# Moving the norm factors of the memory's rows into the second projection chunk of a hybrid decoder layer

## The chip, the cores and the metric

The kernel runs on one core of a Trainium2 chip. Time is device time in microseconds (us). A core has five engines that run side by side, each in the order of its own instructions: TensorE (PE; PEld is its weight load), VectorE (DVE), ScalarE (ACT), GpSimd (POOL) and SyncE (SP), which here only issues DMAs. They wait for each other by semaphores.

## What is computed

One decoder layer on 1024 tokens of width 1024, in float32:

```
h = x + w_out [ DSA-sparse-attention(groupA) ; DiffAttn(groupB) ](rmsnorm(x) @ w_in)
h = h + CrossAttn(rmsnorm(h), rmsnorm(mem))      # 4 heads, 256 memory tokens
h = h + ConvGLU(rmsnorm(h))

def rmsnorm(x, g):
    y = xf * lax.rsqrt(jnp.mean(xf * xf, axis=-1, keepdims=True) + EPS)
    return y * g

def cross_attention(hn, memn, w_xq, w_xk, w_xv, w_xo, g_xq, g_xk):
    k = rmsnorm((memn @ w_xk).reshape(B, M, X_HEADS, X_HEAD_DIM), g_xk)
    v = (memn @ w_xv).reshape(B, M, X_HEADS, X_HEAD_DIM)
```

The memory `mem` has 256 rows of width 1024. What the change is about are the factors 1/sqrt(mean of squares + eps) of these rows, one for each.

## The kernel before

Tokens and memory rows lie 128 to a tile, one on each partition. The input projection runs in column chunks: chunk 0 (0 to 48 us), chunk 1 (to about 106 us; its loop over eight token tiles calls `proj_mm(1, t)` and `c1_post`, `c1_tr`, which build the keys of group A and of the index heads), and chunks 2 to 4 (to about 264 us). Each product is three matmuls, L308 to L310, on a split of the operands, and ScalarE evacuates the sum at L646. The split of a weight tile `raw` is made at L201 and L204.

Then comes the differential attention ("B phase", 264 to 480 us), in units of one head and one block of 128 queries. A unit is a chain over the engines: GpSimd splits the queries (`hl`, L738, L739), TensorE transposes them (L746), ScalarE evacuates (`qbs`, L748), TensorE makes the logits (L766, L767), VectorE masks and takes the maximum (`e`, `st`, L774), ScalarE takes the exponential (L776), VectorE combines the two softmaxes (reciprocal L784, L785, L786), TensorE transposes the result (L691), ScalarE evacuates (`pt`, L682), and TensorE multiplies by the values (L797). Into the units are put the key and value products of the memory (`mem_mm`, L885; evacuation `mem_evac`, L889, which scales by the row factors `rm`; `memk_post` with the Square L894, the reduce L896, `rstd` on VectorE and two products with `gkq` at L900), and steps of the top-k search of group A (L553 on ScalarE, L555 to L571 on VectorE). After it come group A's attention (to 650 us), the cross-attention and the ConvGLU.

Except in the ConvGLU, a scheduler that follows a timeline of its own sets the order of the instructions on each engine; no order is written by hand around the change. Buffers come from rings: `rt("t2")` has three, the pool `early` has five of tag "xr" and closes when tile 2 of chunk 1 is reached. The search steps are issued by `tick` at a pace, behind the last evacuations; that is so in both kernels.

The row factors before: `mem_prep`, called as the B phase opens, loads the two memory tiles of 512 KB (L873) on SP's queue and takes ScalarE's Square with its sum, `ssm` (L875); two loads of the gain vectors (`gx`, L877, L878) follow, whose product `gkq` GpSimd makes (L879). At step -2 of the B loop GpSimd's `rstd` turns `ssm` into `rm` (L107, L108, L118 to L127, twelve steps). VectorE's form of `rstd` has nine (L107 to L116). All of them work on two columns.

Of the kernel before, what the change touches and what calls it, by code (L numbers as in the profile page):

```python
# [9 lines left out]
F32 = mybir.dt.float32  # L10
F32R = mybir.dt.float32r
BF = mybir.dt.bfloat16
I32 = mybir.dt.int32
AF = mybir.ActivationFunctionType
# [4 lines left out]
P = 128  # L19
T = 1024  # L20
D = 1024
# [17 lines left out]
def rows(ap, n=P):  # L39

    return bass.AP(tensor=ap.tensor, offset=ap.offset, ap=[[0, n]] + [list(d) for d in ap.ap])
# [3 lines left out]
def hybrid_layer(ctx, tc, I, out):  # L45
    nc = tc.nc
    pe, act, dve, pool, sp = nc.tensor, nc.scalar, nc.vector, nc.gpsimd, nc.sync

    def open_pool(name, **kw):
        st = ExitStack()  # L50
        p = st.enter_context(tc.tile_pool(name=name, bufs=1, reuse_waits="tile", **kw))
        return st, p
# [8 lines left out]
    def nm(s):  # L61
        cnt[0] += 1
        return f"{s}_{cnt[0]}"

    def ctile(shape, dt, name):
        return const.tile(shape, dt, name=name)
# [10 lines left out]
    def accp():  # L77
        return ps.tile([P, 512], F32, name=nm("acc"), tag="acc", bufs=2)

    def small(name, shape=(P, 8), bufs=8):  # L80
        return wpool.tile(list(shape), F32, name=nm(name), tag=name, bufs=bufs)
# [8 lines left out]
    rm = ctile([P, 2], F32, "rm")  # L90
# [7 lines left out]
    ssm = ctile([P, 2], F32, "ssm")  # L98
# [3 lines left out]
    def rstd(eng, r, ss, n, scale):  # L102


        w = small("rst", (P, 3, 8), 4) if n <= 8 else rt("hl", [P, 3, 64], F32, "rstw")
        m, y, t = w[:, 0, :n], w[:, 1, :n], w[:, 2, :n]
        eng.tensor_scalar(m, ss, scale, EPS, op0=OP.mult, op1=OP.add)  # L107
        eng.tensor_scalar(y.bitcast(I32), m.bitcast(I32), -0.5, 1597463007.0, op0=OP.mult, op1=OP.add)  # L108
        if eng is dve:
            eng.scalar_tensor_tensor(t, y, -3.0 / 16, y, op0=OP.mult, op1=OP.mult)  # L110
            eng.tensor_tensor(t, t, m, op=OP.mult)
            eng.scalar_tensor_tensor(y, t, 9.0 / 16, y, op0=OP.add, op1=OP.mult)
            eng.scalar_tensor_tensor(t, y, 64.0 / 9, y, op0=OP.mult, op1=OP.mult)
            eng.tensor_tensor(t, t, m, op=OP.mult)
            eng.scalar_tensor_tensor(t, t, -10.0 / 3, t, op0=OP.add, op1=OP.mult)
            eng.scalar_tensor_tensor(r, t, 5.0, y, op0=OP.add, op1=OP.mult)  # L116
        else:
            eng.tensor_tensor(t, y, y, op=OP.mult)  # L118
            eng.tensor_tensor(t, t, m, op=OP.mult)
            eng.tensor_scalar(t, t, -3.0 / 16, 9.0 / 16, op0=OP.mult, op1=OP.add)  # L120
            eng.tensor_tensor(y, t, y, op=OP.mult)
            eng.tensor_tensor(t, y, y, op=OP.mult)
            eng.tensor_tensor(t, t, m, op=OP.mult)
            eng.tensor_scalar(m, t, 64.0 / 9, -10.0 / 3, op0=OP.mult, op1=OP.add)
            eng.tensor_tensor(t, t, m, op=OP.mult)
            eng.tensor_scalar(t, t, 64.0 / 9, 5.0, op0=OP.mult, op1=OP.add)
            eng.tensor_tensor(r, t, y, op=OP.mult)  # L127
# [179 lines left out]
    def mm3(o, lh, ll, rh, rl, start, stop):  # L307
        pe.matmul(o, lhsT=lh, rhs=rh, start=start, stop=False)  # L308
        pe.matmul(o, lhsT=lh, rhs=rl, start=False, stop=False)  # L309
        pe.matmul(o, lhsT=ll, rhs=rh, start=False, stop=stop)  # L310
# [13 lines left out]
    def rt(tag, shape, dt, name):  # L324
        return rot.tile(shape, dt, name=nm(name), tag=tag, bufs=ROT[tag])

    ROT = {"X": 3, "t2": 3, "tb": 2, "kk2": 2, "hl": 2, "qt": 2}
    qa_d = tc.dram_tile([T, 512], F32, name="qa_d")
# [11 lines left out]
    early_st, early = open_pool("early")  # L340
    ki_t = [kq([P, T], F32R, "ki") for j in range(2)]

    for tag, n in (("X", 512), ("t2", 512), ("hl", 512), ("tb", 256), ("kk2", 256), ("qt", 128)):
        rt(tag, [P, n], F32, tag)
# [16 lines left out]
    for k in range(KT):  # L361
# [11 lines left out]
        for t in (C1_ORDER if k == KT - 1 else range(NT)):  # L373
            s = slice(t * P, (t + 1) * P)
            mm3(pj0[t][:, :452], h[:, s], l[:, s], w0[k][:, 0, :452], w0[k][:, 1, :452], k == 0, k == KT - 1)
        if k == 0:
# [5 lines left out]
            for j, g in enumerate(("g_ka", "g_qa", "g_qb", "g_kb")):  # L382
                sp.dma_start(gv[:, j, :], rows(I[g]))
            lamv = rt("X", [P, 4, 64], F32, "lamv")
            for j, g in enumerate(("lam_q1", "lam_k1", "lam_q2", "lam_k2")):
# [8 lines left out]
    for t in range(NT):  # L394
        xt = early.tile([P, T], F32, name=nm("xraw"), tag="xr", bufs=5)
        sp.dma_start(xt, I["x"][t * P:(t + 1) * P, :])
        jk = rt("t2", [P, T], BF, "jk")
# [6 lines left out]
    dve.tensor_scalar(gs[:, :, 0:32], gv[:, :, 32:64], -1.0, None, op0=OP.mult)  # L404
    ang = rt("X", [P, NT, 32], F32, "ang")
    kk = rt("hl", [P, NT, 32], F32, "kk")
# [23 lines left out]
    for j in range(2):  # L430
        dve.scalar_tensor_tensor(lt, lamv[:, 2 * j, :], 1.0, lamv[:, 2 * j + 1, :], op0=OP.mult, op1=OP.mult,
                                 accum_out=misc[:, j:j + 1])
# [34 lines left out]
    def c1_evac(t):  # L467
        if t % 2 == 0:
            c1x[t // 2] = early.tile([P, 2, 512], F32, name=nm("c1x"), tag="xr", bufs=5)
        X = c1x[t // 2][:, t % 2, :]  # L470
        act.activation(X[:, :452], pj0[t][:, :452], AF.Copy, scale=rx[:, t:t + 1])
        act.activation(X[:, 452:484].bitcast(BF), X[:, 0:64], AF.Square, accum_out=rka[:, 0, t:t + 1])
# [166 lines left out]
    def proj_mm(c, t):  # L639
        pages = W.get(("in", c), 8)  # L640
        p = accp()
        s = slice(t * P, (t + 1) * P)
        for k in range(KT):
            mm3(p, xh[k][:, s], xl[k][:, s], pages[k][:, 0, :], pages[k][:, 1, :], k == 0, k == KT - 1)
        X = rt("X", [P, 512], F32, "X")
        last["act"] = act.activation(X, p, AF.Copy, scale=rx[:, t:t + 1])  # L646
        return X
# [80 lines left out]
    def b_load_q(u):  # L728
        h, i = b_units[u]
        qt = rt("qt", [P, 2, 64], F32, "qt")  # L730
        sp.dma_start(qt.rearrange("p c d -> p (c d)"), qk_d[h // 2][i * P:(i + 1) * P, (h % 2) * 128:(h % 2) * 128 + 128])
        b_q[u] = qt
# [55 lines left out]
    def b_t(u):  # L788
        h, i = b_units[u]
        b_pt[u] = p_transposes(b_e[u][0][0], i + 1)  # L790
# [21 lines left out]
    store = None  # L812
    idxq = [lambda t=t, h=h: idx_head(t, h) for t in range(2, NT) for h in range(4)]
    mb, sc = {}, {}
    for t in range(NT):
        X = proj_mm(1, t)
        if t == 2:
            early_st.close()
            scp_st, scp = open_pool("scp")
            for i in range(2, NT):  # L820
                mb[i] = scp.tile([P, P * (i + 1)], BF, name=f"mb{i}")
                sc[i] = scp.tile([P, P * (i + 1)], F32, name=f"sc{i}")
        if t == 7:
            W.free(8)
        W.pump(2 if t == 3 else 1)
        for a in steps[t]:
            if a == "i":
                idxq.pop(0)()
            else:
                (c1_post if a[0] == "p" else c1_tr)(int(a[1]))  # L830
        if store:
            store()
        store = proj_post(1, t, X)
# [24 lines left out]
    def etile(name):  # L858
        return obp.tile([P, T], F32, name=nm(name), tag="e", bufs=4)
# [7 lines left out]
    def mem_prep():  # L867
        pages = W.get("memT", 2)
        for j in range(KT):
            mstat[j] = pages[j // 4].bitcast(F32)[:, j % 4 // 2, (j % 2) * 256:(j % 2) * 256 + 256]  # L870
        for t in range(2):
            xt = etile("mtok")
            sp.dma_start(xt, I["mem"][t * P:(t + 1) * P, :])  # L873
            jk = rt("t2", [P, T], BF, "jk")
            act.activation(jk, xt, AF.Square, accum_out=ssm[:, t:t + 1])  # L875
        gx = rt("t2", [P, 2, 256], F32, "gx")
        sp.dma_start(gx[:, 0, :], rows(I["g_xq"]))  # L877
        sp.dma_start(gx[:, 1, :], rows(I["g_xk"]))  # L878
        pool.tensor_tensor(gkq, gx[:, 0, :], gx[:, 1, :], op=OP.mult)  # L879
# [70 lines left out]
    for s in range(-4, NB):  # L950
        h, i = b_units[max(s, 0)]
        m = s % NT

        def ok(u):
            return 0 <= u < NB
        if s % 4 == 0:
            if s >= 0:
                b_acc[s // 4] = accp()
        if s + 5 >= 2 and ok(s + 5):
            b_load_q(s + 5)  # L960
        if s >= 0 and h < 3 and m == 1:
            b_load_k(h + 1)
            b_load_v(h + 1)
        if ok(s + 4):
            b_split(s + 4)
        if s == -2:
            rstd(pool, rm, ssm, 2, 1.0 / D)
        if ok(s + 3):
            b_qt(s + 3)
        if ok(s):  # L970
            b_t(s)
        if ok(s + 2):
            b_s(s + 2)
        mem_step(MB)
        if ok(s + 1):
            b_comb(s + 1)
        if s >= 0 and h < 3 and 2 <= m <= 5:
            b_k(h + 1, (m - 2) // 2, 4 * (m % 2))
        if ok(s):
            b_av(s)  # L980
            W.pump(1)
            tick(0.8 + 0.85 * (i + 1))
# [753 lines left out]
```

## Time and profile before

| what | us |
|---|---|
| median of 3 runs (lowest to highest) | 1662.94 (1659.94 to 1664.27) |
| the profiled execution, its time | 1662.24 |
| the profiled execution, its span | 1660.4 |
| TensorE busy (share) | 1572.2 (95%) |
| VectorE busy (share) | 1208.5 (73%) |
| ScalarE busy (share) | 803.7 (48%) |
| GpSimd busy (share) | 639.1 (38%) |
| granted TensorE clock, mean | 0.978 |

The rows that follow further down come from this one profiled execution. A busy share is an average over stages: the ConvGLU stages keep TensorE full, and its waits lie in the first 480 us. What counts for the change are two stretches, the entry to the B phase (264 to 302 us), where code is taken out, and chunk 1 (50 to 82 us), where it is put in.

### The profile page before, as it was taken

What the parts mean: (1) busy time and instruction counts of PE and PEld (TensorE: products, weight loads), DVE (VectorE), ACT (ScalarE), POOL (GpSimd) and SP (SyncE); (2) the same over time, 40 slices, a digit from 0 to 9 for tenths busy, and PEclk for the clock granted to TensorE, in tenths of its full rate; (3) what the DMA queues carried; (4) which work ended last, traced back from release to release, by engine and by line L of the source; (5) the groups of instructions that cost most, each with busy time, mean ns of one, the idle gap of its engine ahead of it and who ended that gap; (6) DMA issues with size and microseconds to landing.
All of it is one profiled execution on the core that took longest, in us unless ns stands there. A gap on an engine that the chain in (4) does not pass through costs nothing.

```text
span 1660.4 us, 22257 instructions
## 1 busy us (share of the span) xinstructions
PE 1572.2 (95%) x7596; PEld 1271.6 (77%) x7596; DVE 1208.5 (73%) x2356; ACT 803.7 (48%) x1696; POOL 639.1 (38%) x888
## 2 busy tenths in 40 slices
PE   8899898888789999999999997999999999999999
PEld 7788675666668888878777775888887777888887
DVE  5738888878868875345544379989999999855554
ACT  6556665677877446428442265433333333343432
POOL 2735776223351131031101023666666666551111
PEclk9999998989989999999999998999999999999999
DMA  8320236221210122152203121455555555799812
GB/s 284 102 83 32 91 128 216 77 78 47 64 64 27 52 96 70 67 181 102 89 1 114 40 97 57 167 191 179 176 180 180 183 184 179 262 361 366 305 52 76
DMA packets 112162, 220.06 MB, mean 133 GB/s; under 512 B 18480, under 2 KB 38448, under 8 KB 112048
## 3 DMA queue, kind: packets, MB, share of 16 engines
q1 hardware_dynamic: 91072, 148.37, 26.7%
q0 software_dynamic: 18384, 61.36, 10.4%
q10 hardware_dynamic: 2592, 8.91, 1.4%
q8 instruction: 60, 0.98, 0.2%
q14 instruction: 54, 0.44, 0.1%
HBM read 160.92 MB, written 57.67 MB: 132 GB/s over the span
## 4 chain that ended last, share of the span: by engine, by line
PE 68%; DVE 16%; DMA 6%; ACT 4%; issue 3%; POOL 2%; SPq 0%; ACTq 0%; POOLq 0%; DVEq 0%
PE acc L308 11%; PE acc L310 10%; PE acc L309 10%; PE big L309 4%; PE big L308 4%; PE big L310 4%; PE trp L308 3%; PE trp L309 3%; PE trp L310 3%; PE acc L1036 3%; PE acc L885 2%; DVE jk L565 2%; DVE wp L204 2%; PE trp L691 2%; PE big L1275 2%
## 5 line engine op out<-in xcount | busy, mean ns | idle before, releaser
L204 DVE TENSOR_TENSOR wp<-raw,wp 128x512 fp32r<-128x512 f32 (+1 forms) x184 | 186.1, 1021 | 28.1 <-ACT wp L201 17.8
L201 ACT CAST wp<-raw 128x512 fp32r<-128x512 f32 (+1 forms) x184 | 108.3, 614 | 178.0 <-DVE raw L227 121.0
L1600 DVE TENSOR_TENSOR wp<-fo,wp 128x1024 fp32r<-128x1024 f32 x77 | 102.4, 1344 | 76.8 <-ACT wp L1599 69.2
L1549 POOL TENSOR_TENSOR fs<-fs,fs 128x512 f32<-128x512 f32 x88 | 128.5, 1460 | 64.3 <-DMA fs<-u_d 49.1
L1599 ACT CAST wp<-fo 128x1024 fp32r<-128x1024 f32 x77 | 79.8, 1049 | 107.9 <-PE trp L310 43.1
L308 PE MATMUL acc<-wp,xh 128*128 128x512 f32 (+1 forms) x272 | 109.6, 405 | 3.0 <-ACT X L646 3.0
L309 PE MATMUL acc<-wp,xh 128*128 128x512 f32 (+1 forms) x272 | 109.0, 401 | 0.0
L310 PE MATMUL acc<-wp,xl 128*128 128x512 f32 (+1 forms) x272 | 108.7, 400 | 0.0
L553 ACT ACTIVATE mb<-sc,cand 128x384 bf16<-128x384 f32 (+1 forms) x96 | 75.4, 786 | 35.9 <-DVE cand L557 30.5
L203 POOL TENSOR_SCALAR wp<-raw 128x512 fp32r<-128x512 f32 (+1 forms) x36 | 24.5, 685 | 176.8 <-DVE rst L110 63.6
L682 ACT COPY pt<-trp 128x512 f32<-128x512 f32 (+3 forms) x144 | 66.1, 475 | 40.6 <-PE trp L691 40.3
L1036 PEld LDWEIGHTS acc<-va_t,pt 128*128 128x128 f32 x576 | 75.2, 196 | 9.1 <-ACT pt L682 7.2
L1036 PE MATMUL acc<-va_t,pt 128*128 128x65 f32 x576 | 77.8, 274 | 3.7 <-ACT pt L682 3.6
L1646 POOL TENSOR_TENSOR hr<-hr,r 128x512 f32<-128x512 f32 x16 | 26.8, 1691 | 114.6 <-DVE r L1662 62.9
L1018 DVE CUSTOM_DVE_ANT_0 ea<-big,mb,ra 128x384 f32<-128x384 f32 (+5 forms) x48 | 45.4, 945 | 28.7 <-PE trp L691 25.1
L308 PEld LDWEIGHTS acc<-wp,xh 128*128 128x128 f32 x272 | 52.4, 193 | 15.0 <-ACT X L646 3.7
L1497 ACT ACTIVATE fc<-fc 128x1024 f32<-128x1024 f32 x22 | 23.4, 1062 | 82.9 <-DVE fc L1496 82.8
L204 POOL TENSOR_TENSOR wp<-raw,wp 128x512 fp32r<-128x512 f32 x36 | 47.2, 1325 | 40.5 <-ACT wp L201 40.1
L1019 ACT ACTIVATE ea<-ea,sta 128x128 f32<-128x128 f32 (+7 forms) x64 | 49.6, 776 | 25.7 <-DVE sta L1018 23.5
L1494 ACT ACTIVATE fc<-fa,cw 128x1024 f32<-128x1024 f32 x22 | 27.4, 1244 | 71.4 <-DVE fa L1453 71.4
L309 PEld LDWEIGHTS acc<-wp,xh 128*128 128x128 f32 x272 | 52.3, 192 | 11.3 <-issue 0.2
L310 PEld LDWEIGHTS acc<-wp,xl 128*128 128x128 f32 x272 | 52.1, 192 | 11.4
(422 smaller groups left out, 5113.7 us busy)
## 6 DMA issues: line engine op xcount, KB each, us to landing
raw<-in_w_ffn_in_dram SPq DMA_DIRECT2D x44, 512.0 KB, 4.1
fs<-in_w_ffn_out_dram POOLq DMA_DIRECT2D x44, 256.0 KB, 3.5
ws_d<-fs POOLq DMA_DIRECT2D x44, 256.0 KB, 2.3
fs<-u_d POOLq DMA_DIRECT2D x44, 256.0 KB, 3.8
us_d<-fs POOLq DMA_DIRECT2D x44, 256.0 KB, 3.2
fo<-us_d SPq DMA_DIRECT2D x44, 256.0 KB, 5.4
fo<-ws_d SPq DMA_DIRECT2D x44, 256.0 KB, 5.4
u_d<-fg POOLq DMA_DIRECT2D x21, 512.0 KB, 3.7
```

What stands on the lines that cost most here:

```text
L201: act.copy(pg[:, 0, :n], src)
L204: (dve if el == "d" else pool).tensor_tensor(pg[:, 1, :n], src, pg[:, 0, :n].bitcast(F32), op=OP.subtract)
L308: pe.matmul(o, lhsT=lh, rhs=rh, start=start, stop=False)
L309: pe.matmul(o, lhsT=lh, rhs=rl, start=False, stop=False)
L310: pe.matmul(o, lhsT=ll, rhs=rh, start=False, stop=stop)
L553: act.activation(mb[i], sc[i], AF.Sign, bias=cf[:, j:j + 1], scale=-1.0, accum_out=cnt[:, j:j + 1])
L682: act.copy(dst, src)
L1019: last["act"] = act.activation(e[:, :n], e[:, :n], AF.Exp, bias=st[:, 0, h:h + 1], scale=-1.0)
L1036: pe.matmul(acc[:, hh * 65:hh * 65 + 65], lhsT=pt, rhs=va_t[:, kt, :], start=kt == 0, stop=kt == i)
L1549: pool.tensor_tensor(o, p, q, op=op)
L1599: act.copy(hi, raw)
L1600: dve.tensor_tensor(lo, raw, hi.bitcast(F32), op=OP.subtract)
```

## The change

The load, the Square and the rstd of the memory's rows become a function `mem_norm`, called for the first two tiles of chunk 1's loop. The loaded tile comes from the pool `early` (tag "xr") in place of the one that `mem_prep` used, the Square's output still from the ring `t2`. After the second tile VectorE, and not GpSimd, computes `rm`. The rest of `mem_prep` stays.

```
     mb, sc = {}, {}
+
+    def mem_norm(t):
+
+        xt = early.tile([P, T], F32, name=nm("mtok"), tag="xr", bufs=5)
+        sp.dma_start(xt, I["mem"][t * P:(t + 1) * P, :])
+        jk = rt("t2", [P, T], BF, "jk")
+        act.activation(jk, xt, AF.Square, accum_out=ssm[:, t:t + 1])
+        if t == 1:
+            rstd(dve, rm, ssm, 2, 1.0 / D)
+
     for t in range(NT):
         X = proj_mm(1, t)
+        if t < 2:
+            mem_norm(t)
...
             mstat[j] = pages[j // 4].bitcast(F32)[:, j % 4 // 2, (j % 2) * 256:(j % 2) * 256 + 256]
-        for t in range(2):
-            xt = etile("mtok")
-            sp.dma_start(xt, I["mem"][t * P:(t + 1) * P, :])
-            jk = rt("t2", [P, T], BF, "jk")
-            act.activation(jk, xt, AF.Square, accum_out=ssm[:, t:t + 1])
         gx = rt("t2", [P, 2, 256], F32, "gx")
...
-        if s == -2:
-            rstd(pool, rm, ssm, 2, 1.0 / D)
```

Behind the new function the lines of the changed kernel lie 12 lower than before, from the gain vectors on 7, and behind the last place 5.

ScalarE at the entry to the B phase, before (`jk` is the Square of the memory rows, `e` the exponentials, `X` and `sq` the first memory block):

```order
L748 CAST qbs_2778<-trp_2775 128x256
L875 ACTIVATE jk_2731,ssm<-mtok_2729 128x1024
L776 ACTIVATE e_2791,st_2780<-e_2791,st_2780 128x1024
L875 ACTIVATE jk_2735,ssm<-mtok_2733 128x1024
L776 ACTIVATE e_2794,st_2780<-e_2794,st_2780 128x1024
L776 ACTIVATE e_2815,st_2809<-e_2815,st_2809 128x256 x2
L748 CAST qbs_2807<-trp_2804 128x256
L889 ACTIVATE X_2930<-acc_2754,rm 128x512
L894 ACTIVATE sq_2932<-X_2930 128x512
L776 ACTIVATE e_2861,st_2850<-e_2861,st_2850 128x896
```

ScalarE at the same place in the change (L896 is the evacuation, L901 its Square):

```order
L896 ACTIVATE X_2927<-acc_2764,rm 128x512
L748 CAST qbs_2762<-trp_2759 128x256
L748 CAST qbs_2775<-trp_2772 128x256
L901 ACTIVATE sq_2929<-X_2927 128x512
L776 ACTIVATE e_2788,st_2777<-e_2788,st_2777 128x1024
L776 ACTIVATE e_2791,st_2777<-e_2791,st_2777 128x1024
L776 ACTIVATE e_2812,st_2806<-e_2812,st_2806 128x256 x2
L748 CAST qbs_2804<-trp_2801 128x256
L776 ACTIVATE e_2858,st_2847<-e_2858,st_2847 128x896
```

The two Squares between the exponentials are gone, and the evacuation with its Square moved ahead of all four exponentials.

VectorE at the same entry, before, from the combination of the first unit on (`jk` here is a search step, `ss` the block's sum of squares):

```order
L786 SCALAR_TENSOR_TENSOR e_2791<-e_2794,st_2780,e_2791 128x1024
L784 RECIPROCAL st_2809<-st_2809 128x2
L785 SCALAR_TENSOR_TENSOR st_2809<-st_2809,neglam 128x1
L786 SCALAR_TENSOR_TENSOR e_2815<-e_2815,st_2809 128x256
L565 TENSOR_SCALAR jk_2886,ccnt_527<-mb_936,cx_535 128x640
L565 TENSOR_SCALAR jk_2888,ccnt_527<-mb_938,cx_535 128x768
L774 ISA e_2861,st_2850<-big_2851,tri,rqk_76 128x896
L774 ISA st_2850 128x1
L896 TENSOR_REDUCE ss_2934<-sq_2932 128x2
L570 TENSOR_SCALAR crej_531<-ccnt_527 128x2
L774 ISA e_2864,st_2850<-big_2852,tri,rqk_76 128x896
```

VectorE there in the change (the reduce, L903, and the first seven of the nine rstd steps stand further ahead still, between the masks of the first unit and this place; L907 are the two products with `gkq`):

```order
L786 SCALAR_TENSOR_TENSOR e_2788<-e_2791,st_2777,e_2788 128x1024
L115 SCALAR_TENSOR_TENSOR rst_2934<-rst_2934 128x2
L784 RECIPROCAL st_2806<-st_2806 128x2
L116 SCALAR_TENSOR_TENSOR rr_2932<-rst_2934 128x2
L785 SCALAR_TENSOR_TENSOR st_2806<-st_2806,neglam 128x1
L907 SCALAR_TENSOR_TENSOR X_2927<-X_2927,rr_2932,gkq 128x256 x2
L786 SCALAR_TENSOR_TENSOR e_2812<-e_2812,st_2806 128x256
L565 TENSOR_SCALAR jk_2883,ccnt_527<-mb_954,cx_535 128x640
L565 TENSOR_SCALAR jk_2885,ccnt_527<-mb_956,cx_535 128x768
L570 TENSOR_SCALAR crej_531<-ccnt_527 128x2
L571 SCALAR_TENSOR_TENSOR cx_535<-cx_535,crej_531 128x2
L774 ISA e_2858,st_2847<-big_2848,tri,rqk_76 128x896
```

The work on the first memory block and the search step L571 now stand ahead of the mask-and-max of 896 columns.

SP in chunk 1 of the change (`raw` are weight loads, `vb_d` stores of the values; before, the same rows stand without the two loads):

```order
L188 DMA raw_712<-in_w_in_dram 128x2x512
L819 DMA mtok_741<-in_mem_dram 128x1024
L188 DMA raw_751<-in_w_in_dram 128x2x512
L188 DMA raw_865<-in_w_in_dram 128x2x512
L654 DMA vb_d<-X_739 128x512
L819 DMA mtok_845<-in_mem_dram 128x1024
L654 DMA vb_d<-X_843 128x512
L188 DMA raw_1242<-in_w_in_dram 128x2x512
```

The first load stands ahead of one weight load, the second ahead of a store and of chunk 2's first weight load. On ScalarE the Squares stand behind L484 and behind L496, each in front of an evacuation L646; on VectorE the nine steps begin behind L452, two of them ahead of a scaling of keys, L483. On SP at the entry to the B phase the two gain loads stand one place ahead of a query load (L731) that they followed before, and on GpSimd their product stands ahead of that query's split.

## Rows read from the trace of the kernel before

**Rows 1.** Page, part 1, whole span: engine, busy us (share), instructions.
```profile
PE 1572.2 (95%) x7596; PEld 1271.6 (77%) x7596; DVE 1208.5 (73%) x2356; ACT 803.7 (48%) x1696; POOL 639.1 (38%) x888
```

**Rows 2.** Stretches: start:end us, length, busy us by engine, granted clock, DMA share, GB/s.
```profile
264.00:282.00 18.00, 11.25 (x40) 6.07 (x38) 14.10 (x42) 10.15 (x24) 7.29 (x15) 0.91 1.03 346
282.00:289.00 7.00, 5.73 (x18) 4.45 (x19) 6.89 (x15) 3.97 (x10) 6.30 (x16) 0.50 0.53 128
289.00:302.00 13.00, 13.00 (x54) 8.95 (x53) 12.64 (x43) 5.56 (x17) 4.72 (x10) 0.87 0.54 167
264.00:480.00 216.00, 178.37 (x929) 130.81 (x927) 178.82 (x524) 149.55 (x368) 78.08 (x167) 0.94 0.29 89
```

**Rows 3.** Waits, 260 to 300 us: who <- for whom, us, times, longest.
```profile
POOL rst L107 <- ACT jk L875: 7.2, 1, 7.2
...
PE trp L746 <- DVE st L785: 5.1, 1, 5.1
```

**Rows 4.** Chain of waits, 262 to 302 us: start us, us, what.
```profile
266.94 9.95 DMA mtok<-in_mem_dram
276.98 1.15 ACT jk L875 x2
...
279.26 1.04 ACT jk L875 x2
...
287.14 1.13 ACT e L776 x2
...
288.58 1.12 PE trp L691 x4
```

**Rows 5.** Timeline of DVE at the entry: start us, us, operation, [idle before <-releaser].
```profile
278.16 0.48 DVE L774 CUSTOM_DVE_ANT_0 e<-big,tri,rqk 128x256 f32<-128x256 f32 x1 [0.92 <-ACT jk L875]
...
281.46 0.17 DVE L784 RECIPROCAL st<-st 128x2 f32<-128x2 f32 x1 [2.40 <-ACT e L776]
...
285.95 1.15 DVE L774 CUSTOM_DVE_ANT_0 e<-big,tri,rqk 128x896 f32<-128x896 f32 x1
...
287.02 0.68 DVE L896 TENSOR_REDUCE ss<-sq 128x2 f32<-128x512 f32 x1
...
289.08 0.33 DVE L571 SCALAR_TENSOR_TENSOR cx<-cx,crej 128x2 f32<-128x2 f32 x1
289.34 0.51 DVE L108 TENSOR_SCALAR rst<-rst 128x2 int32<-128x2 int32 x1
...
293.25 0.16 DVE L116 SCALAR_TENSOR_TENSOR rr<-rst 128x2 f32<-128x2 f32 x1
...
293.52 0.88 DVE L900 SCALAR_TENSOR_TENSOR X<-X,rr,gkq 128x256 f32<-128x256 f32 x2
```

**Rows 6.** Tiles mtok, gx and (from 40 to 75 us) raw: time to landing.
```profile
DMA to landing us min/median/max: 8.3/9.1/10.0
...
DMA to landing us min/median/max: 4.9/5.2/5.5
...
DMA to landing us min/median/max: 3.6/4.0/4.7
```

**Rows 7.** Timelines of PE, ACT and DVE in chunk 1.
```profile
64.89 0.69 PE L494 MATMUL trp<-ident,kk 128*128 128x128 f32 x2 [4.66 <-DVE kk L483]
...
80.22 0.38 PE L494 MATMUL trp<-ident,kk 128*128 128x128 f32 x2
...
65.62 0.27 ACT L496 CAST ka<-trp 128x128 fp32r<-128x128 f32 x1 [2.99 <-PE trp L494]
...
73.71 0.69 ACT L646 ACTIVATE X<-acc,rx 128x512 f32<-128x512 f32 x1 [2.14 <-PE acc L310]
...
65.87 0.41 DVE L458 TENSOR_TENSOR hl<-c1x,hl 128x256 fp32r<-128x256 f32 x1
...
74.40 0.48 DVE L483 TENSOR_SCALAR kk<-c1x,rka 128x128 f32<-128x128 f32 x1 [0.41 <-PE trp L494]
```

## The prediction

> **What bounds the kernel now.** I read in this order: the busy shares, the stretches around the place that loses code, the longest waits there, the chain of waits, and then the rows of each engine, there and where the code lands. TensorE (PE) is busy for 95% of the span [rows 1], so a change can gain only where it waits. [...] Two long waits stand there, TensorE for a small VectorE (DVE) step, 5.1 us, and GpSimd (POOL) for ScalarE's (ACT's) Square of the memory rows, 7.2 us [rows 3]. The chain says why: the load of the memory rows takes 9.95 us from its issue, and both Squares (1.15 and 1.04 us) run in the chain, among the exponentials [rows 4]. Behind them comes VectorE work, then the exponential at 287.14 (1.13 us), and TensorE's transposes at 288.58 [rows 4]. From 289 to 302 TensorE is busy for all 13.00 us [rows 2]. So whatever is saved at the entry counts only if it moves the transposes at 288.58.
>
> **What is taken out at the entry.** Two loads, two Squares and twelve GpSimd steps go. In the order of the change ScalarE's exponentials follow each other with no Square between, and the evacuation of the first memory block and its Square stand ahead of them. The reciprocal that waited 2.40 us for an exponential [rows 5] then waits for less: two Squares, 1.15 + 1.04 = 2.2 us, lay ahead of it. Its start moves from 281.46 to about 279.3. TensorE's wait of 5.1 us ends about as much earlier; call it 3 us left.
>
> **What takes its place.** VectorE's order decides. Before, the block's reduce, its nine rstd steps, its two gain products and a search step at 289.08 stood at or behind the mask-and-max of 896 columns at 285.95 [rows 5]. Now they stand ahead of it. Their cost: reduce 0.68, search step 0.33, products 0.88 for both, which is 1.89 us; nine rstd steps as 4 x 0.51 and 5 x 0.16 = 2.8 us, when each waits for the one ahead of it (L108 and L116), or 9 x 0.16 = 1.4 when they fill cracks. So 3.3 to 4.7 us are pulled forward, against VectorE idle of 0.92 + 2.40 = 3.3 us that they can fill [rows 5]. The mask-and-max starts between 285.95 and 287.35, plus up to 0.4 of idle that stays. I take 0.7 us later, the middle. The exponential and the transposes of [rows 4] hang on it in that order, so 288.58 becomes about 289.3: **+0.7 us** (0 to +1.8). The stall isn't shortened, it is moved.
>
> [...]
>
> **What VectorE has in hand afterwards.** The 3.3 us of work done early are no longer queued behind 289. From 264 to 480 VectorE is busy 178.82 of 216 us and TensorE 178.37 [rows 2], so TensorE waits 37.6 us there, a part of it on VectorE. Until 302 the lead is worth nothing, since TensorE is full. Behind that it is worth between 0 and 3.3 us; I take half: **-1.6 us**.
>
> **The clock.** After the wait of 5.1 us TensorE ran at 0.50 until 289, and from 289 to 302 the mean is 0.87 [rows 2]. If that mean is a mix of 0.50 and 1.00, 26% or 3.4 us were at half, which cost 1.7 us. With the wait split into one of some 3 us and one of 3 to 4 us in front of the transposes, I count a fifth of this back: **-0.3** (bounds -1.7 and +1).
>
> **The gain vectors.** Their two loads now stand ahead of a query load on SP's queue, and their product ahead of that query's split on GpSimd. They land 4.9 to 5.5 us after issue [rows 6]. If they go out at about 273, when a tile of VectorE's comes free, they land by 278.5; the product is done by 279.3, two small GpSimd steps follow, and TensorE's transposes behind the wait of 5.1 us can start at 280. Cost nothing, covered by the wait that remains. With the 10.0 us that the memory load took [rows 6] they land at 283; the products on VectorE are then late too, and the transposes slip by about 2 us more. That is inside my range.
>
> **What is put in at chunk 1.** Two loads of 512 KB. Weight loads of that size there land in 3.6 to 4.7 us, the memory loads at the entry took 8.3 to 10.0 [rows 6]; I take 4.7, as the queue's other loads there are few. The first load goes out at about 51 and its Square stands on ScalarE in front of idle time of 2.99 us [rows 7]: 1.06 + 0.19 us, hidden. The second needs a slot that VectorE's step at 65.87 reads last [rows 7], so it goes out at about 66.4 and lands by 71.2. It also holds the store and the weight load queued behind it on SP for some 2 us; that weight is for the next chunk. Its Square stands in front of the evacuation at 73.71, which had 2.14 us idle ahead of it [rows 7]: ends at 72.5, hidden. Nine rstd steps then run on VectorE from about 73. Two of them stand ahead of the scaled keys at 74.40, whose transposes TensorE starts at 80.22 [rows 7]: 5.3 us of cover against at most 2 x 0.5. The other seven lie behind. Cost: **0**. Without the cover it is a TensorE wait such as that of 4.66 us at 64.89 [rows 7], which is the third rival.
>
> **Other moves.** A few search products and transposes stand one to six matmuls (0.2 us each) away from where they stood, and several search steps trade places. Price 0, bounds -3 and +3.
>
> **Sum.** +0.7 - 1.6 - 0.3 + 0 = -1.2 us. The profiled execution took 1662.24 us, 0.70 below the median 1662.94, so 1661.0 on its scale and **1661.7 us** as a median: no change that counts. A measurement of this kernel tells about 0.3%, 5 us, from no change.
>
> **Rivals.** *First, the whole stall goes.* The pulled-forward steps all slip into idle time, the transposes at 288.58 move with the exponentials by 2.2 us, all 1.7 us of half clock come back, and VectorE's lead of 3.3 us passes to the end: 7.2 us, 1655.7. For it: the wait that falls away is real and in the chain. Against it: the order has VectorE's extra steps ahead of the mask-and-max, and 3.3 to 4.7 us don't fit well into 3.3. [...]
>
> *Second, the entry isn't what the time hangs on.* Both ends of the entry's terms cancel, and what is left are the moves elsewhere: 1662.9, give or take 3. For it: TensorE's 95%, and FFN stages in which nothing changes. Against it: VectorE's idle of 3.3 us does get filled.
>
> *Third, slower: the second memory load comes late in chunk 1.* If it takes 10.0 us, as the memory loads of [rows 6], it lands at 76.5, and its Square holds the evacuation of 73.71 until 77.8, four us late; the rstd steps hold the scaled keys on VectorE until about 79.3, still ahead of 80.22. Past a landing of about 11 us, or if TensorE has no second accumulator free, TensorE waits: 4 us, and then up to 3.5 more while it runs at half clock, as from 282 to 289 [rows 2]: +6 us, 1669. For it: the load waits for a slot, and SP's queue behind it too. Against it: loads of this size in this stretch landed in 4.7 us at most.
>
> **How the numbers follow.** Forecast 0.53, first rival 0.21, second 0.13, third 0.13. Of the forecast's share 0.04 is faster by more than 0.3% and 0.03 slower; of the first rival 0.17 is faster and 0.04 within; the second is within; of the third 0.11 is slower and 0.02 within. So faster 0.21, within 0.3% 0.65, slower 0.14. The range is 1654 to 1667.5: it holds the first rival, with some room below it, and the second, and leaves out most of the third.
>
> **What would show it.** Right: no Square and no load of memory rows at the entry; TensorE's wait there some 3 us, and a second one in front of the transposes near 289; the mask-and-max of 896 columns at 286 to 287.5, just behind the products; chunk 1 with its waits as before. The first rival: transposes near 286.4 and a clock near 1.00 from 280 on. The third: a ScalarE wait on the memory load near 72, and a new TensorE wait near 78 to 82. I am wrong if the span from 302 on changes by more than 3 us, for which I have no mechanism.

## The result: slower, and the loss lies more than 700 us behind the change

The changed kernel takes 1672.62 us (median of 7 runs, 1666.09 to 1678.37), the kernel before 1662.94 us (median of 7 beside it, 1659.94 to 1668.57). The ratio is 1.0062, with a 95% interval from 1.0042 to 1.0082: **slower by 0.6%, some 10 us**. The forecast was 1661.7 us and no change, with a range up to 1667.5. The span of the profiled execution is 1671.7 us, and it took 1673.50 us.

The page of the changed kernel, part 1, answers to [rows 1]:

```profile
PE 1569.3 (94%) x7596; PEld 1268.4 (76%) x7596; DVE 1202.6 (72%) x2365; ACT 803.0 (48%) x1696; POOL 640.1 (38%) x876
```

TensorE has no more work than before; it waits more. To find where, I set the start of the same instruction in both traces side by side (the numbers are the start in the change less the start before, in us):

| instruction | before | change |
|---|---|---|
| an evacuation of the projection, L646 | 163.8 | 0.0 |
| two evacuations on, L646 | 182.4 | -1.5 |
| last evacuation of the projection, L646 | 264.8 | -1.7 |
| evacuation of the second memory block, L889 | 299.5 | -2.0 |
| evacuation of the last memory block, L889 | 475.9 | -3.8 |
| first gate multiply of the ConvGLU, L1502 | 1042.8 | -4.7 |
| fifth gate multiply | 1120.6 | -4.7 |
| twentieth gate multiply | 1423.7 | +3.8 |
| twenty-first, the last on GpSimd | 1444.9 | +11.0 |
| last sum of output products on VectorE, L1664 | 1633.5 | +11.3 |

So the change is ahead until 1120 us. Then 8.5 us are lost bit by bit between 1120 and 1424, and 7.2 us at once between 1424 and 1445.

Two cautions on the lead. The 1.7 us at 264.8 are not the entry's: 1.5 of them come between 164 and 182 us, in the projection, where no line of the diff stands. Of the five kernels of the experiments that have the loads and Squares in chunk 1, four show the same step, 1.4 to 1.5 us; the three in which nothing is changed ahead of the ConvGLU do not. Why it is there stays open. And the 4.7 us at 1043 us can't be told from scatter: those three kernels are ahead of this trace of before by 2.0, 3.0 and 4.8 us there, though nothing up to that point differs.

**The entry to the B phase in the change.** Stretches (columns as in [rows 2], set 2 us earlier, since the change arrives 1.7 us earlier):

```profile
262.00:280.00 18.00, 11.50 (x41) 6.29 (x39) 17.42 (x54) 9.71 (x23) 7.43 (x12) 0.96 1.00 326
280.00:287.00 7.00, 4.57 (x14) 3.69 (x15) 6.67 (x14) 1.05 (x2) 5.93 (x12) 0.50 0.24 69
287.00:300.00 13.00, 12.99 (x59) 8.59 (x58) 10.98 (x35) 6.74 (x20) 3.26 (x6) 0.93 0.48 158
```

VectorE, which worked 14.10 us in the first stretch [rows 2], now works 17.42: its idle time is filled. TensorE gains next to nothing there, and its granted clock is again 0.50 behind the wait. The longest waits (columns as in [rows 3]) and the instructions that count on VectorE and TensorE:

```profile
POOL gkq L886 <- DMA gx<-in_g_xk_dram: 7.2, 1, 7.2
PE trp L746 <- POOL hl L739: 7.2, 2, 6.1
```

```profile
277.51 0.17 DVE L784 RECIPROCAL st<-st 128x2 f32<-128x2 f32 x1
...
280.63 1.51 DVE L907 SCALAR_TENSOR_TENSOR X<-X,rr,gkq 128x256 f32<-128x256 f32 x2
...
285.14 1.14 DVE L774 CUSTOM_DVE_ANT_0 e<-big,tri,rqk 128x896 f32<-128x896 f32 x1
```

```profile
281.92 0.69 PE L746 MATMUL trp<-ident,hl 128*128 128x128 f32 x2 [6.13 <-POOL hl L739]
...
286.70 2.19 PE L691 MATMUL trp<-ident,e 128*128 128x128 f32 x8
...
289.21 1.11 PE L797 MATMUL acc<-vb,pt 128*128 128x128 f32 x8
```

The Squares and their wait of [rows 3] are gone, and TensorE's wait has grown from 5.1 to 6.1 us. GpSimd stands in front of the gain vectors' product for 7.2 us, and the query split is queued behind it. The loads landed as expected, but the order has two `kdup` steps (L721, 0.6 us each) between the two halves of the split, so the transposes of the queries (L746) came at 281.92 and not at 280. From there on TensorE works without a wait, but for 0.5 us ahead of 283.12: the transposes of the result (L691) follow at 286.70, all eight in one row, and the values' product (L797) stands behind them. Before, the second four of them waited, for an evacuation (`qbs`, L748) that stood behind the exponential of 287.14 on ScalarE:

```profile
288.58 1.12 PE L691 MATMUL trp<-ident,e 128*128 128x128 f32 x4 [0.80 <-ACT qbs L748]
...
290.25 2.02 PE L797 MATMUL acc<-vb,pt 128*128 128x128 f32 x8
```

That wait is gone. In the change the query split, and not the mask or the exponential, sets when the values' product starts.

**Chunk 1 in the change** (the landing of the two loads, the Squares on ScalarE, the scaled keys on VectorE):

```profile
DMA to landing us min/median/max: 4.1/4.6/5.1
```

```profile
61.49 1.05 ACT L821 ACTIVATE jk<-mtok 128x1024 bf16<-128x1024 f32 x1
...
71.02 1.06 ACT L821 ACTIVATE jk<-mtok 128x1024 bf16<-128x1024 f32 x1
...
73.48 0.69 ACT L646 ACTIVATE X<-acc,rx 128x512 f32<-128x512 f32 x1 [1.31 <-PE acc L310]
```

```profile
74.17 0.33 DVE L483 TENSOR_SCALAR kk<-c1x,rka 128x128 f32<-128x128 f32 x1 [0.42 <-PE trp L494]
```

All of it is hidden: the evacuation of 73.71 [rows 7] now starts at 73.48 and still waits for TensorE, and the keys are scaled at 74.17, before 74.40. TensorE's only wait from 50 to 107 us, for scaled keys (L494), is 4.0 us long, against 4.7 before.

**The ConvGLU.** Stretch 1080 to 1420 us, first before, then in the change (these rows of before were not shown above), and VectorE's wait that grew most:

```profile
1080.00:1420.00 340.00, 335.53 (x1429) 266.61 (x1428) 311.58 (x336) 108.46 (x166) 219.28 (x237) 1.00 0.53 181
```

```profile
1080.00:1420.00 340.00, 329.45 (x1397) 260.82 (x1396) 295.28 (x329) 105.78 (x163) 216.33 (x229) 1.00 0.52 177
```

```profile
DVE ws L225 <- DMA raw<-in_w_ffn_in_dram: 12.6, 15, 1.9
```

```profile
DVE ws L225 <- DMA raw<-in_w_ffn_in_dram: 27.8, 14, 3.5
```

L225 is the first sum on a weight tile of 512 KB; VectorE waits for that load 12.6 us before, 27.8 in the change. TensorE is fed by VectorE's sums (L1453, in the change L1458), and its waits for them add up to 4.3 us before and 10.3 in the change. Most of the 8.5 us is there. VectorE's longer wait is no measure of the loss, for in the same rows VectorE works 16.3 us less (311.58 and 295.28). The diff touches nothing here. What is different is GpSimd's order. GpSimd makes the gate multiply of each of the 21 blocks (L1502, L1507 in the change) and between them, with its own loads and stores, sums of the output weights and of the gated activations. (The part ahead of the prediction sets the ConvGLU apart, as if the scheduler left it alone. In the code only TensorE's order is fixed by hand, and only up to the first block; GpSimd's order in the ConvGLU is the scheduler's.) One block, before, with the loads that SyncE issues and VectorE's split and first sum behind GpSimd's rows:

```profile
1281.99 0.55 POOL L1545 DMA_DIRECT2D fs<-u_d  x1
1282.56 2.42 POOL L1502 TENSOR_TENSOR fg<-fc,fg 128x1024 f32<-128x1024 f32 x1
1284.90 0.58 POOL L1545 DMA_DIRECT2D fs<-in_w_ffn_out_dram  x1
...
1281.72 4.17 SPq L188 DMA_DIRECT2D raw<-in_w_ffn_in_dram  x2
...
1282.21 3.32 DVE L204 TENSOR_TENSOR wp<-raw,wp 128x512 fp32r<-128x512 f32 x1
1286.34 0.69 DVE L225 TENSOR_TENSOR ws<-raw 128x512 f32<-128x512 f32 x1 [0.81 <-DMA raw<-in_w_ffn_in_dram]
```

And the same block in the change:

```profile
1281.66 0.55 POOL L1550 DMA_DIRECT2D fs<-u_d  x1
1282.20 0.55 POOL L1550 DMA_DIRECT2D fs<-in_w_ffn_out_dram  x1
1282.77 2.42 POOL L1507 TENSOR_TENSOR fg<-fc,fg 128x1024 f32<-128x1024 f32 x1
...
1281.39 1.53 SPq L188 DMA_DIRECT2D raw<-in_w_ffn_in_dram  x2
...
1281.88 0.68 DVE L204 TENSOR_TENSOR wp<-raw,wp 128x512 fp32r<-128x512 f32 x1
1286.01 0.69 DVE L225 TENSOR_TENSOR ws<-raw 128x512 f32<-128x512 f32 x1 [3.45 <-DMA raw<-in_w_ffn_in_dram]
```

The second load has changed places with the multiply. It goes out 2.7 us earlier, and its issue, 0.55 us, holds the multiply back until VectorE's split (L204) is over. Beside the multiply that split took 3.32 us; now it takes 0.68, and VectorE waits for the load instead. The sum L225 comes no later for it: it starts 4.62 us behind the issue of its load in both kernels. But the split frees a weight buffer, and so SyncE's next load of 512 KB goes out 1.2 us behind the first, where it was 3.8 (the rows of SPq hold two issues of 0.33 us each). It meets the first one and two loads of GpSimd, and lands 6.8 us after its issue. Of TensorE's waits in this stretch 4.4 us lie in the four blocks in which that happens, and the rest, 5.9 us, is not far from the 4.3 of before.

The last block is another matter. Before, its multiply ran at 1444.92; in the change it stands behind a store and two loads, and each of the loads waits for an earlier store to land:

```profile
1453.98 0.55 POOL L1550 DMA_DIRECT2D fs<-u_d  x1 [1.44 <-DMA us_d<-fs]
1455.38 0.55 POOL L1550 DMA_DIRECT2D fs<-in_w_ffn_out_dram  x1 [0.84 <-DMA us_d<-fs]
1455.94 2.35 POOL L1507 TENSOR_TENSOR fg<-fc,fg 128x1024 f32<-128x1024 f32 x1
```

```profile
ACT fc L1499 <- POOL fg L1507: 10.3, 1, 10.3
...
PE acc L308 <- DVE fg L1458: 6.4, 1, 6.4
```

The multiply frees a buffer of the ring that ScalarE's next block needs (four buffers); ScalarE waits 10.3 us for it, VectorE for ScalarE, and TensorE 6.4 us for VectorE.

### The profile page after: what moved, and what is told of

Same layout as the page of the kernel before. It is cut to its first block, busy times and chain, and to the rows that moved or that the text cites. A ratio compares the mean times of both kernels' runs of the same rounds, so it can differ in the third digit from the quotient of the medians.

```text
span 1671.7 us, 22259 instructions
## 1 busy us (share of the span) xinstructions
PE 1569.3 (94%) x7596; PEld 1268.4 (76%) x7596; DVE 1202.6 (72%) x2365; ACT 803.0 (48%) x1696; POOL 640.1 (38%) x876
## 4 chain that ended last, share of the span: by engine, by line
PE 47%; DVE 28%; DMA 10%; POOL 5%; ACT 5%; issue 5%; SPq 0%; ACTq 0%; DVEq 0%; POOLq 0%
PE acc L308 8%; PE acc L310 8%; PE acc L309 8%; DVE wp L204 4%; DMA raw<-in_w_ffn_in_dram 2%; DVE jk L565 2%; PE big L309 2%; PE acc L1041 2%; PE big L310 2%; PE big L308 2%; DMA fs<-u_d 2%; POOL fs L1554 2%; DVE fc L1501 2%; PE trp L691 2%; PE big L1280 2%
## 5 line engine op out<-in xcount | busy, mean ns | idle before, releaser
L204 DVE TENSOR_TENSOR wp<-raw,wp 128x512 fp32r<-128x512 f32 (+1 forms) x184 | 172.9, 950 | 28.4 <-ACT wp L201 18.0
L1502 ACT ACTIVATE fc<-fc 128x1024 f32<-128x1024 f32 x22 | 23.4, 1062 | 89.8 <-DVE fc L1501 89.8
L1023 DVE CUSTOM_DVE_ANT_0 ea<-big,mb,ra 128x384 f32<-128x384 f32 (+5 forms) x48 | 45.4, 945 | 27.9 <-PE trp L691 24.9
L204 POOL TENSOR_TENSOR wp<-raw,wp 128x512 fp32r<-128x512 f32 x36 | 47.4, 1331 | 39.5 <-ACT wp L201 39.1
```

The costliest lines, as they stand in the source:

```text
L204: (dve if el == "d" else pool).tensor_tensor(pg[:, 1, :n], src, pg[:, 0, :n].bitcast(F32), op=OP.subtract)
```

## The experiments

The theory that these rows suggest: the loss comes from where the scheduler put GpSimd's multiplies in the ConvGLU, and has nothing to do with the norm factors as such. The rival: something else in the later stages, on the other engines or in the phase of the DMAs, and GpSimd's row only follows. Written as G multiply, U its store, l load, t sum, s store of a sum, the steady row of two blocks is

```
before:  G l t U s l l t s t s t s l   G t U s l l l t s t s t s l
change:  G t U s l l t s t s t s l     G t U s l l l t s t s t s l l
```

All times are set against runs of the kernel before that were made beside them (medians 1661.83 us for the first four, 1661.36 for the others).

**GpSimd's row of before in the changed kernel.** A list of letters chains GpSimd's instructions in the ConvGLU; each edge, of class `NoSync`, is there for the order alone. `row` collects the instructions as they are traced.

```
+    ROW = "lllGtUststslGUtsllltststGsllU..."    # the order of before
+    line = [row[k].pop(0) for k in ROW]
+    for i, j in zip(line, line[1:]):
+        tc.add_manual_dep(j, i.name, mybir.DependencyInfo(
+            mybir.DependencyClass.NoSync, mybir.DependencyReason.DATA), reason="row")
```

> The changed kernel, with the order of GpSimd's instructions in the ConvGLU chained by hand to that of the kernel before; the norm factors stay in chunk 1. Row theory (the 16 us lost behind 1000 us come from where GpSimd's gate multiplies stand among the loads and stores of the sums): the gain of about 5 us that the trace of the change shows at 920 us is kept, so about 1657.5 us, 0.3% faster than before, range 1655 to 1660. Rival (the loss comes from what runs on the other engines, or from the DMAs' phase against them, and GpSimd's row only follows): about 1672, as the change.

Measured: 1660.12 us, ratio 0.9989 (0.9974 to 1.0005). The loss is gone. VectorE's wait in 1080 to 1420 is that of before again:

```profile
DVE ws L225 <- DMA raw<-in_w_ffn_in_dram: 11.1, 16, 1.9
```

The rival falls: up to the last blocks of the ConvGLU VectorE, ScalarE and SyncE keep the order of the change in this run, and only GpSimd's row is exchanged. But the gain that is left is 0.1%, 1.7 us, not the 5 us that I expected, and its interval touches no change: the lead of 4.7 us in one trace was in part the luck of that execution.

**GpSimd's row of the change in the kernel before.** The same lines with the letters of the change; the norm factors are where they were.

> The kernel before, with the order of GpSimd's instructions in the ConvGLU chained by hand to that of the change; nothing of the norm factors is moved. Row theory: it loses what the change loses there, some 13 to 16 us, so 1676 to 1679 us, and is the same as before up to 1000 us. Rival (the cause is the moved norm work, or other engines' order): 1663 us.

Measured: 1674.39 us, ratio 1.0066 (1.0044 to 1.0087), the whole loss without the change. GpSimd's row is that of the change to the letter here; VectorE's order moves by one place in six blocks. VectorE's wait and the last block:

```profile
DVE ws L225 <- DMA raw<-in_w_ffn_in_dram: 29.1, 16, 3.6
```

```profile
ACT fc L1495 <- POOL fg L1503: 7.5, 1, 7.5
```

**Only the last multiply put back**, and **only the steady row put back**, both in the changed kernel, by the letters alone:

```
 last multiply:   ...l t s t s t [G] s l l U t s...    the rest as in the change
 steady row:      ...l t s t s t s l l [G] U t s...    the rest as before
```

> The changed kernel, with GpSimd's row in the ConvGLU as in the change but for the last gate multiply on GpSimd, which stands ahead of one store and two loads as before. Row theory with two separate parts: the wait of 6.4 us near 1450 goes, so 1665 to 1666 us; the drift of about 8 us between 1080 and 1420 stays. If the last multiply is all of it: 1657.5. If it is none: 1672.

> The changed kernel, with GpSimd's row in the ConvGLU as before for all gate multiplies but the last, which stands behind one store and two loads as in the change. Row theory with two separate parts: the drift of about 8 us goes, the wait near 1450 stays, so 1664 to 1666 us. If the steady row is all of it: 1657.5. If it is none: 1672.

Measured: 1667.30 us, 1.0026 (1.0006 to 1.0045), and 1665.19 us, 1.0021 (1.0001 to 1.0041). Neither is all of it. From 0.9989 with both put back, the steady row costs 0.37% and the last multiply 0.32%, together 0.69%; the change against that row costs 0.73%. The two parts add up, as far as intervals of 0.2% either way can tell. In the traces VectorE's wait is 24.0 us with the steady row of the change and 11.2 with that of before. That it doesn't measure the loss shows here too: the execution traced with 24.0 us was the fastest of its ten, 1658.59 us. For the last multiply ScalarE's wait is no sign either, since with the row of before put back ScalarE can wait 6.0 us for a multiply that is early:

```profile
ACT fc L1500 <- POOL fg L1508: 6.0, 1, 6.0
...
PE acc L308 <- DVE fg L1459: 1.4, 1, 1.4
```

TensorE's wait behind it tells the kernels apart: 6.4, 3.8 and 3.1 us in the three traces in which the multiply is late, 1.4 us here and none in the other traces in which it is early.

**Why the steady row costs: an extra load at the same place.** The theory is that the moved load contends with SyncE's loads; the rival, that the multiply costs by its own place. The kernel before with its own row, and one more DMA of 256 KB that nobody reads, in 8 blocks; once just ahead of the multiply, where the change has its load, once 10 us later in the same blocks.

```
+            if f in [4, 6, 8, 10, 12, 14, 16, 18]:
+                row["x"].append(pool.dma_start(xtra[f * P:(f + 1) * P, :],
+                                               I["w_ffn_out"][f * P:(f + 1) * P, 0:512]).ins)
 at the multiply:  x G l t U s l l t s t s t s l
 elsewhere:        G l t U s l l t s x t s t s l
```

> The kernel before, GpSimd's ConvGLU row as it was, plus an extra DMA of 256 KB that nobody reads (8 in all, memory to memory), issued just ahead of the gate multiply in every second block, where the change has its weight load of the sums. Contention theory (the moved load lands on top of the 512 KB weight load that VectorE's first sum waits for): VectorE's wait for that load grows from 12.6 us to 20 us or more between 1080 and 1420, and the time by 4 to 8 us, 1666 to 1670. Position theory (the multiply itself being later costs it): 0.6 us a block on GpSimd at most and no VectorE wait, 1662 to 1664.

> The same 8 extra DMAs in the same blocks, issued some 10 us later in the block, behind the first store of the weight sums. Contention theory: they meet no load that VectorE waits for at once, VectorE's wait stays near 12.6 us and the time within 2 us of 1663. If any extra traffic costs: as the extra load at the multiply, 1666 to 1670.

Measured: 1666.60 us, 1.0027 (1.0018 to 1.0037), at the multiply, and 1663.58 us, 1.0014 (1.0003 to 1.0025), elsewhere. VectorE's wait, at the multiply and then elsewhere:

```profile
DVE ws L225 <- DMA raw<-in_w_ffn_in_dram: 25.7, 15, 3.9
```

```profile
DVE ws L225 <- DMA raw<-in_w_ffn_in_dram: 10.5, 12, 1.9
```

The wait follows the place of the load, as the theory said. But these two runs don't separate it from the rival: the issue of the extra load takes GpSimd 0.55 us ahead of the multiply, so here too the multiply comes behind VectorE's split, which is over in 0.68 us (at 1283.02) as in the change. What speaks for contention is the landing. From 1080 to 1420 us 16 loads of 512 KB go out 1.2 us behind another with two loads of GpSimd between: four in the change, five with its row in the kernel before, three with only the last multiply put back, four with the extra load at the multiply, none in the other traces. They land in 6.2 to 7.8 us, all others in 5.6 at most. Whether the landing alone makes TensorE wait is not shown. For the time it is less clean still. The extra traffic costs 2 us elsewhere too, and the two intervals overlap, so of the 0.37% this shows a part; and executions differ much (1658.59 to 1674.46 us in the run with only the last multiply put back).

**The entry: the gain vectors behind the query split.** The changed kernel with GpSimd's row of before, and

```
-        gx = rt("t2", [P, 2, 256], F32, "gx")      # in mem_prep, with its loads and gkq
+        if s == -2:                                # in the B loop
+            gx = rt("t2", [P, 2, 256], F32, "gx")
```

> The changed kernel with GpSimd's ConvGLU row of before, and the product of the gain vectors traced at step -2 of the B loop, so that it stands behind the query split on GpSimd and no longer ahead of it. If TensorE's wait of 6.1 us at the entry (split behind product, product behind the gain loads) sets the entry: the wait shrinks by 1.5 to 2 us, the transposes behind it and the end follow, 1658 us. If VectorE's queue sets it (block products and search step ahead of the mask of 896 columns): that mask stays within 0.5 us of 285.1 against the start of the entry, and the time stays at 1660 us, as with the row of before alone.

Measured: 1660.32 us, 0.9989 (0.9979 to 0.9999), the same as with the row of before alone. TensorE's wait did shrink by 1.9 us:

```profile
280.02 0.69 PE L746 MATMUL trp<-ident,hl 128*128 128x128 f32 x2 [4.21 <-DVE st L785]
...
288.60 1.23 PE L797 MATMUL acc<-vb,pt 128*128 128x128 f32 x8
```

The values' product starts at 288.60, against 289.21 in the change: of 1.9 us, 0.6 arrive. The mask of 896 columns came at 283.42, earlier than I had said, because here a search step stands behind it, and the second one at 285.43; yet TensorE waits again, for 1.1 us until 285.66, and what it waits for is the next query split on GpSimd (L739), between whose halves a `kdup` step stands. So it isn't VectorE's queue that takes over, and with 1.9 us less of one wait the end doesn't move by anything that can be measured. The first expectation had the wait right and the end wrong; the second had the time right for a reason that doesn't hold.

**The rstd on GpSimd.** As with the row of before, but the twelve steps of GpSimd in place of VectorE's nine.

```
+            rstd(pool, rm, ssm, 2, 1.0 / D)    # at s == -2, as before; not in mem_norm
```

> The changed kernel with GpSimd's ConvGLU row of before, and the twelve rstd steps of the memory rows on GpSimd as before the change, traced at step -2 of the B loop (the scheduler puts them behind chunk 1, as their input is there); loads and Squares stay in chunk 1. If VectorE's nine steps in chunk 1 are hidden, as the trace of the change reads: no difference from the row of before alone, 1660 us, and the same start of the entry within 0.5 us. If they cost: 1 to 2 us faster up to 264 us.

Measured: 1663.20 us, 1.0005 (0.9993 to 1.0017). It isn't faster, and its entry begins 1.0 us later than that of the change, not earlier: VectorE's steps in chunk 1 cost nothing that can be seen. The expected 1660 us and the same start within 0.5 us are missed, though. What this kernel lacks is the step of 1.5 us between 164 and 182 us: it is 0.7 us ahead of the kernel before at either end.

## Why the prediction was wrong

By its own steps:

- **What is taken out.** Right. The reciprocal starts at 277.51; the change arrives 1.7 us earlier, so that is 2.2 us earlier against 281.46 [rows 5], as the two Squares said.
- **What takes its place.** The number came out, the mechanism did not. The mask of 896 columns starts 0.8 us earlier, which against the 1.7 is 0.9 later (0.7 was forecast). The values' product, behind the transposes, starts 1.0 us earlier (289.21 against 290.25), so the stretch from 264 us to there is 0.7 us longer, as forecast; in five traces with the change's entry it is 25.7 to 26.5 us long, in four with that of before 24.9 to 25.6. But the transposes didn't hang on the mask and its exponential: they stood behind the query split. That the two gave the same 0.7 us is luck. One cost was read wrongly too. The steps of 0.51 us [rows 5] are not steps that wait for the one ahead: L110, L111 and L112 take 0.15 to 0.16 us in a row at 277.00 in the change. They are steps beside work of GpSimd. In the trace of before the 184 steps of these lines with GpSimd idle take 0.23 us at most, and the 54 that have GpSimd at work for over half of their time 0.36 at the median and up to 1.27.
- **The gain vectors.** Wrong. "Cost nothing" held for the loads, which landed in 5.2 us, but the steps between the product and the second half of the split weren't counted; TensorE waited 6.1 us where I said 3, and this wait became the gate of the entry. Without it the values' product comes 0.6 us earlier, and the time is the same.
- **What VectorE has in hand.** Not shown. From -1.0 us at the values' product the lead goes to -3.8 at 476 us in one trace, but the three kernels in which nothing is changed ahead of the ConvGLU stand between -0.5 and +2.8 us there and between -2.0 and -4.8 at 1043, against the trace of before.
- **The clock.** TensorE is back at a granted clock of 1.00 sooner than said (from 289 to 292 us it reads 1.00, where it read 0.50 before): the mean behind the entry is 0.93 against 0.87 [rows 2], and the eight matmuls of the values' product take 1.11 us against 2.02. But in those three kernels they take 1.11 too. What [rows 2] show there is the one execution and not the kernel. That a shorter wait at the entry brings back the 1.7 us of half clock, as the first rival counts, no run shows: behind the shortest, 4.21 us with the gain vectors late, matmuls of 512 columns still took 0.63 us, against 0.40 ahead of it.
- **Chunk 1.** Right for chunk 1: landings of 4.1 to 5.1 us, both Squares hidden, no wait of TensorE added. The third rival, which was slower for this reason, didn't come about. The 1.5 us that the change gains between 164 and 182 us have no term in the sum.
- **The sum of these**, -1.2 us, is met by the changed kernel once GpSimd's row in the ConvGLU is put back: 0.9989, -1.8 us (-4.3 to +0.8). That is no proof of its terms: of what the traces repeat, 1.5 us come from a step that it lacks, and 0.7 us are lost at the entry by another gate.
- **Other moves.** This is the step that failed: "Price 0, bounds -3 and +3", with the second rival's "FFN stages in which nothing changes". Instructions do change places there. The scheduler lays its order along one timeline, the earlier part of that timeline had changed, and 700 us on it settled on another row for GpSimd, of which one pair of instructions in every second block and one multiply at the end are all that counts. That costs 0.7%, some 12 us. The prediction's own sign of being wrong, a span from 302 us on that changes by more than 3 us, stands in the table: from -2.0 to +11.3. I read the new order where the code had moved and gave the rest a price by the distance moved ("one to six matmuls"), not by what stands there: a multiply that frees a buffer, behind loads that wait for stores, on an engine whose queue TensorE hangs on three steps later.

What stays open: why the scheduler's row flips, which is in its own timeline and not on the chip; why the change gains 1.5 us between 164 and 182 us; and how the 0.37% of the steady row split between the late landing of the second load and the position of the multiply.

## What to carry to other kernels

Where a scheduler sets the order, an edit's cost isn't bounded by the place of the edit: compare the new order with the old one over the whole program, and price each exchanged pair by what its engine waits for there and who waits for it. A result that doesn't fit the edit is best tried by putting the old order back by hand at the place where the traces part, and the new order into the old kernel; two runs then tell the edit from its side effect. A wait that has grown is not yet a loss: look whether the engine works that much less ahead of it, and follow the wait to the engine that bounds the kernel. And an order that matters, such as a multiply that frees a buffer ahead of loads that wait, is worth fixing in the code.

## What was not expected of the hardware

From 1080 to 1420 us a load of 512 KB lands in 4.1 to 4.3 us at the median in all of these kernels, and in 5.6 at most, unless it goes out 1.2 us behind another one with two loads of 256 KB between: then it takes 6.2 to 7.8 us, though the DMA share over the stretch is 0.52 to 0.54 everywhere. In these traces it is which transfers meet that tells the loads apart, not the mean. A split of VectorE on 512 columns (L204) took 0.68 us where it was over before GpSimd's multiply of 2.42 us began, and 3.32 beside it. And TensorE was slower behind waits of 6.1, 5.1 and 4.2 us alike: matmuls of 512 columns took 0.63 us behind each of them, against 0.40 ahead, and behind the first two the granted clock reads 0.50.
